# A second norm computed earlier, a weight form queued sooner, and a 32-byte shift moved from one product unit to another

## The chip, the cores and the metric

The kernel runs on one core of a Trainium2 chip. A core has five engines with queues of their own: PE (TensorE, matrix products), DVE (VectorE), ACT (ScalarE), POOL (GpSimd) and SP (SyncE, which here issues DMAs). Each works through its instructions in the order of the program and waits at semaphores for the others. The metric is the device time of one execution in microseconds (us), as a median of several runs.

## The reference

One decoder block in float32, 512 tokens by 1024 features: a gated linear attention and a sparse attention in parallel, merged and added to the input, and then the channel mixer. The change lies in the channel mixer and in the norm ahead of it:

```python
x = x + rms_norm(mixed @ w_out[l], norm_mix_post[l])
h = rms_norm(x, norm_ffn_pre[l])                      # the "second norm"
f = (jax.nn.silu(h @ w_ffn_gate[l]) * (h @ w_ffn_up[l])) @ w_ffn_down[l]
x = x + rms_norm(f, norm_ffn_post[l])
```

`w_ffn_gate` and `w_ffn_up` have 2816 columns, 22 blocks of 128.

## The kernel before

Every float32 operand of a product is split into a high part (rounded by a cast) and a low part (the rest), and a product is three matmuls: high by high, high by low, low by high. Features lie on the partitions, in eight tiles k = 0 to 7; tokens lie on the free axis, in two halves e = 0 and 1 of 256.

**The second norm.** `resid(e)` adds the mixers' output to the input. For each k VectorE multiplies (L1424, one input in PSUM) and adds (L1425), ScalarE makes the high part (L1426) and VectorE the low part (L1427). `resid_squares(e)` then squares each tile on ScalarE (L1436) and adds the eight squares up on GpSimd (L1439). `norm2_sums(e)` sums over the partitions with two matmuls of one column (L251; the trace shows each float32 one as two), turns the mean into a reciprocal root on VectorE (L259) and GpSimd (L260), and `norm2_scale(e)` spreads it over the partitions by matmuls (L268) and copies it to `rb_x` on ScalarE (L1450). `normed(e)` multiplies the tiles by it on VectorE (L1608, eight instructions).

**Column blocks 0 to 2, "plain".** The first two (weights `w0` and `w1`, gate and up) run in halves of tokens by `ffn_half` (L1462 to L1464, 48 matmuls for a half), since the products with the unscaled `x` need no norm: the scale is applied behind them. The third uses all 512 tokens at once (L226 to L228, accumulators `third`).

**Column blocks 3 to 21, "units".** From N0 = 3 on a unit replaces the 8 half-size products of a block by 7 (a Strassen-like scheme): a11, s2, s3, s1, a12, a22, s4, named after their weights, each 4 x 3 = 12 matmuls of 256 columns (L1662). VectorE adds the results (L1668, into `us` and `wk`). The weights of a11 and a12 are the gate's two halves (`prep_g`), that of a22 the up's second half (`prep_u`), s1 to s4 are sums of quarters. Their high parts are cast on ScalarE, and the low parts are made by a negated copy and a DMA on GpSimd's queue that adds the weight from memory (`dma_split`). The other operands are `b11`, `b12`, `b21`, `b22` (half e of `nb`) and four differences of them, split by `x_form` (L1617). N0 and N0+1 have only two banks each, of two regions; the matmuls of s1 write the same bank as those of s2, from which the first L1668 reads.

A scheduler puts the instructions in order on each engine, from its own costs and from the places in the program; `tc.issue_after(x)` keeps an instruction behind another one, which may be on another engine. `SHIFT` is 16 and `TURN` 8 elements of four bytes: they set the addresses at which a form of weights begins.

The lines of the program that set the order here are these (before):

```python
    high_end, _ = resid(1, marks[-1])
    ffn_half(0, w0, first, range(5, 8))
    resid_squares(1, range(KD), None, high_end)
    ...
    normed(0)
    x_form("b11", [(b11, *at(0))])
    ffn_half(1, w1, second, range(0, 6))
    scale_made = norm2_sums(1)
    ffn_half(1, w1, second, range(6, 8))
```

Of the kernel before, what the change touches and what calls it, by code (L numbers as in the profile page):

```python
# [11 lines left out]
AF = mybir.ActivationFunctionType  # L12
OP = mybir.AluOpType
# [5 lines left out]
KD = D // 128  # L19
# [14 lines left out]
SHIFT = 16  # L34
TURN = 8
# [98 lines left out]
def hybrid_block_kernel(ctx: ExitStack, tc: tile.TileContext, I, outT):  # L134
    nc = tc.nc
    act, dve, pool, pe = nc.scalar, nc.vector, nc.gpsimd, nc.tensor
# [29 lines left out]
    g_fpre, g_fpost = vecs[:, 16:24], vecs[:, 24:32]  # L166
# [5 lines left out]
    rb_x = base.tile([128, S], F32, name="rb_x")  # L172
# [25 lines left out]
    for key in with_gla + with_cmp + with_att + late:  # L198
        kind, n = key
# [19 lines left out]
    def prod(ps, w, xh, xl, k0, kn, ktot, t=ALL):  # L219

        wh, wl = w
        marks = []
        for kk in range(kn):
            k = k0 + kk
            c = slice(kk * 128, (kk + 1) * 128)
            pe.matmul(ps[:, t], wh[:, c], xh(k)[:, t], start=(k == 0), stop=False)  # L226
            pe.matmul(ps[:, t], wh[:, c], xl(k)[:, t], start=False, stop=False)  # L227
            marks.append(pe.matmul(ps[:, t], wl[:, c], xh(k)[:, t], start=False, stop=(k == ktot - 1)))  # L228
        return marks
# [32 lines left out]
    broadcast, queued = [], {}  # L262
# [13 lines left out]
    for k in range(KD):  # L276
# [3 lines left out]
        if k == 0:  # L280
            act.activation(out=warm, in_=mhalf[:, 0:1], func=AF.Exp)
        last = act.activation(out=hT[:, k, :], in_=X[:, k], func=AF.Copy, scale=g_pre[:, k:k + 1])
        dve.scalar_tensor_tensor(out=hTl[:, k, :], in0=X[:, k], scalar=g_pre[:, k:k + 1],
                                 in1=hT[:, k, :].bitcast(F32), op0=OP.mult, op1=OP.subtract)
# [48 lines left out]
    halves = (slice(0, S // 2), slice(S // 2, S))  # L333
# [205 lines left out]
    for c in range(4):  # L539
        w = tk.next(("tok", 0, c))  # L540
# [78 lines left out]
    for j in range(NP):  # L619
# [6 lines left out]
        after = queued["dve"]  # L626
# [713 lines left out]
    def uu_half():  # L1340
        uturn[0] += 1
        return uub[:, 0:1024] if uturn[0] % 2 else uub[:, 1024:2048]
# [6 lines left out]
    def w_slot(which, shift=SHIFT):  # L1349

        if which == "w":
            return regions.next(shift)
        if which == "c":
            t = hlc(F32R, "w_hl")
            return [t[:, c:c + 1024] for c in (SHIFT, 1024 + SHIFT)]
        if which == "u":
            return uu_half(), uu_half()
        if which in ("d0", "d1"):
            t = wpair(which)
            return t[:, 0:1024], t[:, 1024:2048]  # L1360
        return tuple(wtile(t) for t in {"g3": ("g3h", "g3l"), "rw": ("rw", "rw")}[which])
# [6 lines left out]
    h2h, h2l = quads("h2h", 4, F32R, "hh"), quads("h2l", 2, F32R, "hl")  # L1368
    h2l23 = hlc(F32R, "h2l23")[:, 0:2048].rearrange("p (b a t) -> p b a t", b=2, a=2)
    h2l += [h2l23[:, i] for i in range(2)]  # L1370
    x1 = [slot(k) for k in range(8)]
# [41 lines left out]
    def resid(e, after=None, ks=range(KD), mult_after=None):  # L1413

        t = halves[e]
        if e not in rb_of:
            rb_of[e] = over_partitions(rs1, "tp", blocks[e], after)
        rb = rb_of[e]
        for k in ks:
            i, j = k // 2, k % 2  # L1420
            y = x1[k][:, t]
            hi, lo = h2h[i][:, j, t], h2l[i][:, j, t]
            with tc.issue_after(mult_after.ins) if mult_after else nullcontext():
                dve.tensor_tensor(out=y, in0=y, in1=rb[:, t], op=OP.mult)  # L1424
            dve.tensor_tensor(out=y, in0=y, in1=xs[i][:, j, t], op=OP.add)  # L1425
            last = act.activation(out=hi, in_=y, func=AF.Copy, scale=g_fpre[:, k:k + 1])  # L1426
            end = dve.scalar_tensor_tensor(out=lo, in0=y, scalar=g_fpre[:, k:k + 1], in1=hi.bitcast(F32),  # L1427
                                           op0=OP.mult, op1=OP.subtract)
        return last, end

    def resid_squares(e, ks=range(KD), after=None, squared_after=None):
        t = halves[e]
        for k in ks:
            sq = sq2[0][:, t] if k == 0 else sq2[1 + (k - 1) % 6 // 2][:, halves[(k - 1) % 2]]
            with tc.issue_after(squared_after.ins) if squared_after else nullcontext():
                act.activation(out=sq, in_=x1[k][:, t], func=AF.Square)  # L1436
            if k > 0:
                with tc.issue_after(after.ins) if after else nullcontext():
                    pool.tensor_tensor(out=sq2[0][:, t], in0=sq2[0][:, t], in1=sq, op=OP.add)  # L1439

    rs2 = ffn.tile([128, NT], F32, name="rs2")

# [5 lines left out]
    def norm2_scale(e, after):  # L1448
        ps = over_partitions(rs2, "tp", blocks[e], after)
        return act.copy(rb_x[:, halves[e]], ps[:, halves[e]])  # L1450

    def ffn_half(e, w, ps, ks=range(KD)):

        t = halves[e]
        marks = []
        for k in ks:
            i, j = k // 2, k % 2
            c = slice(k * 128, (k + 1) * 128)
            for x in range(2):
                wh, wl = w[x]  # L1460
                o = ps[x][:, t]
                pe.matmul(o, wh[:, c], h2h[i][:, j, t], start=(k == 0), stop=False)  # L1462
                pe.matmul(o, wh[:, c], h2l[i][:, j, t], start=False, stop=False)
                last = pe.matmul(o, wl[:, c], h2h[i][:, j, t], start=False, stop=(k == KD - 1))  # L1464
            marks.append(last)
        return marks
# [34 lines left out]
    N0 = NPLAIN  # L1501
# [29 lines left out]
        return minus  # L1531

    def prep_g(n, after=None):
        hi, lo = w_slot(("w", "g3", "w")[(n - N0) % 3], SHIFT + (TURN if n == N0 + 3 else 0))
        minus = dma_split(n, hi, lo, raws[n, "w_gate"], I["w_gate"][n], after)
        forms[n, "a11"], forms[n, "a12"] = [(hi[:, c], lo[:, c]) for c in (slice(0, 512), slice(512, 1024))]
        return minus

    def prep_u(n, after=None, t=None):
        t = uu_half() if t is None else t  # L1540
        hi, lo = t[:, 0:512], t[:, 512:1024]
        dma_split(n, hi, lo, ups[n][:, 512:1024], I["w_up"][n, :, 512:1024], after)
        forms[n, "a22"] = (hi, lo)
# [59 lines left out]

    XF = {}

    def normed(e):
        for k in range(KD):
            dve.scalar_tensor_tensor(out=nb[k // 4][e][:, k % 4, :], in0=x1[k][:, halves[e]], scalar=g_fpre[:, k:k + 1],  # L1608
                                     in1=rb_x[:, halves[e]], op0=OP.mult, op1=OP.mult)

    def x_form(name, segs, after=None):

# [144 lines left out]
    for n in (6, 7):  # L1757
        out_half(n, 1)
    sq2 = [t[:, i, :] for t in quads("sq2_", 2, F32, "e") for i in range(2)]
# [4 lines left out]
    on_act, on_dve = resid(0, None, range(KD - 1, KD), queued["mean"])  # L1764
    resid_squares(0, range(3, KD), root)
    marks = ffn_half(0, w0, first, range(3, 5))
    high_end, _ = resid(1, marks[-1])
    ffn_half(0, w0, first, range(5, 8))
    resid_squares(1, range(KD), None, high_end)
    split_pair(N0, s12, ("s1", "s2"), on_act, True)  # L1770
    w1 = (st.next(("g", 1)), st.next(("u", 1)))
    second = (bank("mm"), bank("mm"))
# [3 lines left out]
    marks = ffn_half(1, w0, first, range(0, 2))  # L1776
    norm2_scale(0, marks[-1])
    ffn_half(1, w0, first, range(2, 8))
    nb = [[ffn.tile([128, 4, 256], F32, tag="a%d" % (2 * p + e), name="nb%d%d" % (p, e)) for e in range(2)]
          for p in range(2)]  # L1780
    b11, b12, b21, b22 = [t.rearrange("p q t -> p (q t)") for t in (nb[0][0], nb[0][1], nb[1][0], nb[1][1])]
    normed(0)
    x_form("b11", [(b11, *at(0))])
    ffn_half(1, w1, second, range(0, 6))
    scale_made = norm2_sums(1)
    ffn_half(1, w1, second, range(6, 8))
    third = (bank("acc"), bank("acc"))

    def h2(p):
        return lambda k: p[k // 2][:, k % 2, :]  # L1790

    w2 = st.next(("g", 2))
    marks = prod(third[0], w2, h2(h2h), h2(h2l), 0, 3, KD)
    rb_made = norm2_scale(1, marks[-1])
    x_form("b21", [(b21, flat(quad("e0", F32R, "x4h")), flat(quad("e1", F32R, "x4l")))])
    normed(1)
    prod(third[0], [x[:, 384:1024] for x in w2], h2(h2h), h2(h2l), 3, 5, KD)
# [19 lines left out]
    for n in range(N0, KF):  # L1817
        if n + 2 < KF:
            load(n + 2, "w_gate")
            load(n + 2, "w_up")  # L1820
        last = unit(n, rest_of_forms if n == N0 else None,
                    (lambda copied: prep_u(N0 + 2, copied, uu_next)) if n == N0 + 2 else None)
        if n == N0:
            end = last
        if n == N0 + 1:
            plain_end()
            plain_out(2, *third)()
        if n + 1 < KF:
            prep_st(n + 1, end, plain_outs if n == N0 else None)
        if n + 2 < KF:  # L1830
            prep_g(n + 2, {N0 + 1: queued.get("s1cast"), N0 + 2: queued.get(("s34", N0 + 2)),
                           N0 + 3: queued.get(("s12", N0 + 4))}.get(n))
            if n == N0 + 1:
                uu_next = uu_half()
            if n > N0:
                prep_u(n + 2, queued["s1cast"] if n == N0 + 1 else None)
        if 2 * KH <= n < 2 * KH + 4:
            down_t3(n - 2 * KH)
# [352 lines left out]
```

## Time and profile before

| what | value |
|---|---|
| median of 3 runs | 822.71 us (822.53 to 822.76) |
| the profiled execution's own time | 822.37 us |
| its span, first to last instruction | 820.6 us |
| granted TensorE clock | 1.000 |
| w1's second half begins on PE | 497.26 us |
| first unit (N0) begins on PE | 514.71 us |
| N0+4 begins on PE | 554.83 us |

A row of the timeline gives the start and the length in us, the engine, the line, the operation, the tiles written and read, the shape, how many instructions were merged, and in square brackets how long the engine was idle just before and what released it. The length of a matmul includes its way through the array; what counts for the time is the distance from one start to the next. Line numbers in the profile and below are those of the kernel before, unless they are said to be those of after.

### The profile page before, as it was taken

How to read it: one execution, taken by the hardware profiler on the slowest of the kernel's cores; microseconds unless marked ns; L12 is line 12 of the kernel's file. 1: busy time of each engine (PE TensorE's matmuls, PEld its weight loads, DVE VectorE, ACT ScalarE, POOL GpSimd, SP SyncE). 2: the span in 40 equal slices, each digit the busy share in tenths (PEclk: the TensorE clock that was granted, in tenths of full speed). 3: DMA queues.
4: the chain of work that ended last, by engine and by line, in shares of the span. 5: the costliest groups of instructions: out<-in, count | busy, mean ns of one | idle time of the engine just before them, and what ended most of it. 6: DMA issues, size and time to landing. Idle time of an engine off the chain costs nothing.

```text
span 820.6 us, 14977 instructions
## 1 busy us (share of the span) xinstructions
PE 813.5 (99%) x5676; PEld 750.2 (91%) x5676; DVE 649.5 (79%) x1219; ACT 523.6 (64%) x954; POOL 177.4 (22%) x221
## 2 busy tenths in 40 slices
PE   9999999999999999999999999999999999999997
PEld 8999999988888888888888999999999999889996
DVE  7878889955678988877675387997888778939885
ACT  7666697646536778887545577677655667536453
POOL 0242222312311111111001355012211110001264
PEclk9999999999999999999999999999999999999999
DMA  7588888411233354444238759589788882335323
GB/s 259 139 219 205 183 182 191 103 52 51 92 125 98 96 116 119 111 105 103 55 110 303 227 125 259 102 229 224 185 192 193 199 196 67 101 92 181 91 103 103
DMA packets 45449, 120.75 MB, mean 147 GB/s; under 512 B 5981, under 2 KB 11373, under 8 KB 45249
## 3 DMA queue, kind: packets, MB, share of 16 engines
q1 hardware_dynamic: 30576, 82.40, 30.1%
q0 software_dynamic: 14080, 36.76, 25.4%
q8 instruction: 44, 0.72, 0.3%
q10 hardware_dynamic: 720, 0.64, 0.2%
q14 instruction: 29, 0.23, 0.1%
HBM read 105.10 MB, written 4.19 MB: 133 GB/s over the span
## 4 chain that ended last, share of the span: by engine, by line
PE 93%; DVE 3%; ACT 2%; issue 1%; DMA 0%; SPq 0%; DVEq 0%; ACTq 0%
PE ps_sc L1662 7%; PE ps_mm L226 7%; PE ps_mm L227 6%; PE ps_mm L228 6%; PE ps_acc L1662 5%; PE ps_mm L1662 4%; PE ps_mm L446 4%; PE ps_tp L446 4%; PE ps_tp L1662 4%; PE ps_sc L1993 4%; PE ps_sc L446 3%; PE ps_acc L446 3%; PE ps_tp L1172 2%; PE ps_mm L1993 2%; PE ps_sc L227 1%; PE ps_sc L228 1%
## 5 line engine op out<-in xcount | busy, mean ns | idle before, releaser
L99 ACT CAST wbuf<-wraw 128x1024 fp32r<-128x1024 f32 (+3 forms) x56 | 54.1, 967 | 45.2 <-issue 11.1
L226 PE MATMUL ps_mm<-hT_hi,wbuf 128*128 128x512 f32 x152 | 61.8, 407 | 0.0
L106 DVE TENSOR_TENSOR wbuf<-wraw,wbuf 128x1024 fp32r<-128x1024 f32 (+3 forms) x41 | 44.3, 1082 | 20.6 <-ACT wbuf L99 16.3
L227 PE MATMUL ps_mm<-hT_lo,wbuf 128*128 128x512 f32 x152 | 60.0, 394 | 0.0
L228 PE MATMUL ps_mm<-hT_hi,wbuf 128*128 128x512 f32 x152 | 59.8, 394 | 0.0
L1548 ACT CAST w_d<-s 128x1024 fp32r<-128x1024 f32 x25 | 26.1, 1045 | 30.3 <-PE ps_acc L1662 13.9
L1131 ACT ACTIVATE p<-p,mx 128x512 f32<-128x512 f32 (+1 forms) x64 | 35.8, 560 | 9.2 <-DVE mx L1129 8.4
L244 DVE TENSOR_TENSOR pl<-ps_tp,ph 128x512 fp32r<-128x512 f32 (+1 forms) x64 | 31.2, 490 | 9.7 <-ACT ph L243 8.8
L1129 DVE CUSTOM_DVE_ANT_0 p<-ps_sc,causal 128x512 f32<-128x512 f32 (+1 forms) x64 | 30.0, 485 | 7.4 <-PE ps_sc L1122 7.2
L228 PEld LDWEIGHTS ps_mm<-hT_hi,wbuf 128*128 128x128 f32 x152 | 28.5, 188 | 6.5 <-DVE wbuf L106 0.4
L226 PEld LDWEIGHTS ps_mm<-hT_hi,wbuf 128*128 128x128 f32 x152 | 28.6, 188 | 5.5
L103 POOL DMA_DIRECT2D wbuf<-wraw x15 | 13.1, 875 | 94.3 <-ACT wbuf L102 94.3
L227 PEld LDWEIGHTS ps_mm<-hT_lo,wbuf 128*128 128x128 f32 x152 | 28.7, 189 | 4.5
L1530 POOL DMA_DIRECT2D wbuf<-in_w_gate x13 | 11.1, 856 | 89.1 <-ACT wbuf L1528 71.8
L243 ACT CAST ph<-ps_tp 128x512 fp32r<-128x512 f32 (+1 forms) x64 | 26.4, 414 | 6.1 <-PE ps_tp L1172 5.3
L1555 DVE TENSOR_TENSOR w_d<-s,w_d 128x1024 fp32r<-128x1024 f32 x24 | 29.3, 1220 | 0.0
L1172 PE MATMUL ps_tp<-ident,p 128*128 128x128 f32 x160 | 27.7, 272 | 0.0
L1172 PEld LDWEIGHTS ps_tp<-ident,p 128*128 128x128 f32 x160 | 20.8, 140 | 7.1
L226 PE MATMUL ps_mm<-gla_hi,wbuf 128*128 128x512 f32 x64 | 26.1, 407 | 0.0
L227 PE MATMUL ps_mm<-gla_lo,wbuf 128*128 128x512 f32 x64 | 25.2, 393 | 0.0
L228 PE MATMUL ps_mm<-gla_hi,wbuf 128*128 128x512 f32 x64 | 25.1, 393 | 0.0
L1548 ACT CAST w_hl<-s 128x1024 fp32r<-128x1024 f32 x11 | 11.5, 1046 | 18.2 <-PE ps_acc L1662 7.0
(981 smaller groups left out, 3210.5 us busy)
## 6 DMA issues: line engine op xcount, KB each, us to landing
wraw<-in_w_t SPq DMA_DIRECT2D x28, 512.0 KB, 3.6
wraw<-in_w_gate SPq DMA_DIRECT2D x21, 512.0 KB, 5.6
rw<-in_w_up SPq DMA_DIRECT2D x19, 512.0 KB, 6.7
wbuf<-wraw POOLq DMA_DIRECT2D x15, 512.0 KB, 4.5
wbuf<-in_w_gate POOLq DMA_DIRECT2D x13, 512.0 KB, 5.5
urw<-in_w_t SPq DMA_DIRECT2D x12, 512.0 KB, 5.5
uub<-in_w_up POOLq DMA_DIRECT2D x19, 256.0 KB, 7.3
raw<-in_w_down SPq DMA_DIRECT2D x10, 448.0 KB, 3.3
```

Source lines behind the costliest of these rows:

```text
L99: self.cast = self.nc.scalar.copy(hi[:, :cols], raw[:, :cols])
L106: self.nc.vector.tensor_tensor(out=lo[:, :cols], in0=raw[:, :cols], in1=hi[:, :cols].bitcast(F32), op=OP.subtract)
L226: pe.matmul(ps[:, t], wh[:, c], xh(k)[:, t], start=(k == 0), stop=False)
L227: pe.matmul(ps[:, t], wh[:, c], xl(k)[:, t], start=False, stop=False)
L228: marks.append(pe.matmul(ps[:, t], wl[:, c], xh(k)[:, t], start=False, stop=(k == ktot - 1)))
L244: return dve.tensor_tensor(out=lo, in0=src, in1=hi.bitcast(F32), op=OP.subtract)
L446: pe.matmul(o, w[:, c], x_of(b, q, low), start=(first and q == 0 and i == 0), stop=(q == 3 and i == 2), skip_group_check=True)
L1131: act.activation(out=o, in_=o, func=AF.Exp, scale=-1.0, bias=mx[:, i:i + 1], accum_out=z[:, i:i + 1])
L1172: queued["turn"] = pe.transpose(tp[:, i * 128:(i + 1) * 128], p[:, OFF[i] + k * 128:OFF[i] + (k + 1) * 128], ident)
L1548: cast = act.copy(hi, t)
L1662: last = pe.matmul(o, w[:, c], x[q], start=(first and q == 0 and i == 0), stop=(q == 3 and i == 2), skip_group_check=True)
L1993: pe.matmul(o, c, x[q], start=(first and n == 0 and i == 0), stop=(n == KH - 1 and i == 2), skip_group_check=True)
```

## The change

1. `resid_squares(1, ...)` becomes `second_squares(low_end)`. ScalarE squares tiles 0 to 3 right behind the sixth high part, and tiles 4 to 7 behind the eighth. GpSimd adds three of the squares in place of seven; VectorE adds the other four (three adds L1451 and a last one L1453 in the changed kernel), behind the last low part of `resid(1)`; `normed(0)` comes behind these.
2. The sums `norm2_sums(1)` stand ahead of w1's second half (before: behind six of its eight tiles), and `norm2_scale(1)` behind three of its tiles (before: behind three tiles of the third block).
3. The form a22 of N0+2 is asked for in unit N0+1, behind its copy of the first product, and not in unit N0+2.
4. The gate's form of N0 begins 32 bytes further, and that of N0+3 no longer does.

```diff
@@ resid
-            last = act.activation(out=hi, in_=y, func=AF.Copy, scale=g_fpre[:, k:k + 1])
+            last = queued["high", e, k] = act.activation(out=hi, in_=y, func=AF.Copy, scale=g_fpre[:, k:k + 1])
...
+    def second_squares(low_end):
+        t = halves[1]
+        sq = [sq2[0][:, t]] + [sq2[1 + (k - 1) % 6 // 2][:, halves[(k - 1) % 2]] for k in range(1, KD)]
+        for k in range(KD):
+            with tc.issue_after(queued["high", 1, 5 if k < 4 else 7].ins):
+                act.activation(out=sq[k], in_=x1[k][:, t], func=AF.Square)
+            if 0 < k < 4:
+                pool.tensor_tensor(out=sq[0], in0=sq[0], in1=sq[k], op=OP.add)
+            elif k > 4:
+                with tc.issue_after(low_end.ins):
+                    low_end = dve.tensor_tensor(out=sq[4], in0=sq[4], in1=sq[k], op=OP.add)
+        with tc.issue_after(low_end.ins):
+            queued["squares"] = dve.tensor_tensor(out=sq[0], in0=sq[0], in1=sq[4], op=OP.add)
...
-        hi, lo = w_slot(("w", "g3", "w")[(n - N0) % 3], SHIFT + (TURN if n == N0 + 3 else 0))
+        hi, lo = w_slot(("w", "g3", "w")[(n - N0) % 3], SHIFT + (TURN if n == N0 else 0))
...
-    def prep_u(n, after=None, t=None):
-        t = uu_half() if t is None else t
+    def prep_u(n, after=None):
+        t = uu_half()
...
-    high_end, _ = resid(1, marks[-1])
+    _, low_end = resid(1, marks[-1])
     ffn_half(0, w0, first, range(5, 8))
-    resid_squares(1, range(KD), None, high_end)
+    second_squares(low_end)
...
-    normed(0)
+    normed(0, queued["squares"])
     x_form("b11", [(b11, *at(0))])
-    ffn_half(1, w1, second, range(0, 6))
     scale_made = norm2_sums(1)
-    ffn_half(1, w1, second, range(6, 8))
+    marks = ffn_half(1, w1, second, range(0, 3))
+    rb_made = norm2_scale(1, marks[-1])
+    ffn_half(1, w1, second, range(3, 8))
...
-    marks = prod(third[0], w2, h2(h2h), h2(h2l), 0, 3, KD)
-    rb_made = norm2_scale(1, marks[-1])
+    prod(third[0], w2, h2(h2h), h2(h2l), 0, 3, KD)
...
-                    (lambda copied: prep_u(N0 + 2, copied, uu_next)) if n == N0 + 2 else None)
+                    (lambda copied: prep_u(N0 + 2, copied)) if n == N0 + 1 else None)
...
-            if n == N0 + 1:
-                uu_next = uu_half()
```

The order on VectorE from the end of `resid(1)` to the sums' mean (L259), before. The tiles `slot` hold the sum with the input, `h2l` its low part, `sq` the squares, `nb` the normed tiles, `rs` the mean:

```order
L1427 SCALAR_TENSOR_TENSOR h2l_4804<-slot_4812,vecs,h2h_4801 128x256
L1608 SCALAR_TENSOR_TENSOR nb_5531<-slot_4805,vecs,rb_x 128x256
L1608 SCALAR_TENSOR_TENSOR nb_5531<-slot_4806,vecs,rb_x 128x256
L1608 SCALAR_TENSOR_TENSOR nb_5531<-slot_4807,vecs,rb_x 128x256
L1608 SCALAR_TENSOR_TENSOR nb_5531<-slot_4808,vecs,rb_x 128x256
L1608 SCALAR_TENSOR_TENSOR nb_5533<-slot_4809,vecs,rb_x 128x256
L1608 SCALAR_TENSOR_TENSOR nb_5533<-slot_4810,vecs,rb_x 128x256
L1608 SCALAR_TENSOR_TENSOR nb_5533<-slot_4811,vecs,rb_x 128x256
L1608 SCALAR_TENSOR_TENSOR nb_5533<-slot_4812,vecs,rb_x 128x256
L1617 TENSOR_TENSOR hT_lo<-nb_5531,hT_hi 128x1024
L259 TENSOR_SCALAR rs_4943<-ps_tp 128x2
```

And after, the same stretch (L1623 is `normed`, L1632 `x_form` in the changed kernel):

```order
L1427 SCALAR_TENSOR_TENSOR h2l_4804<-slot_4812,vecs,h2h_4801 128x256
L1451 TENSOR_TENSOR sq_1_5282<-sq_1_5282 128x256 x2
L1451 TENSOR_TENSOR sq_1_5282<-sq_1_5282,sq_0_5281 128x256
L1453 TENSOR_TENSOR sq_0_5281<-sq_0_5281,sq_1_5282 128x256
L1623 SCALAR_TENSOR_TENSOR nb_5531<-slot_4805,vecs,rb_x 128x256
L1623 SCALAR_TENSOR_TENSOR nb_5531<-slot_4806,vecs,rb_x 128x256
L1623 SCALAR_TENSOR_TENSOR nb_5531<-slot_4807,vecs,rb_x 128x256
L1623 SCALAR_TENSOR_TENSOR nb_5531<-slot_4808,vecs,rb_x 128x256
L1623 SCALAR_TENSOR_TENSOR nb_5533<-slot_4809,vecs,rb_x 128x256
L1623 SCALAR_TENSOR_TENSOR nb_5533<-slot_4810,vecs,rb_x 128x256
L1623 SCALAR_TENSOR_TENSOR nb_5533<-slot_4811,vecs,rb_x 128x256
L259 TENSOR_SCALAR rs_4943<-ps_tp 128x2
```

Four adds have come between the low part and the norm's first half, and L259 has moved ahead of the norm's last tile and of the first split of `b11`.

VectorE around N0's first additions, before (`w_d` and `s` belong to weight forms; `x_1`, `x_3` and `x5l` are low parts of the last two other operands, for a22 and s4):

```order
L1617 TENSOR_TENSOR hT_lo<-nb_5531,hT_hi 128x1024
L1668 TENSOR_TENSOR us<-ps_tp,us 128x256
L1617 TENSOR_TENSOR x5l<-nb_5533,x5h 128x1024
L1668 TENSOR_TENSOR us<-ps_tp,us 128x256
L1617 TENSOR_TENSOR x_1_5771<-nb_5534,x_0_5770 128x512
L1617 TENSOR_TENSOR x_3_5773<-nb_5534,x_2_5772 128x512
L1668 TENSOR_TENSOR wk<-ps_tp,us 128x256
L1564 TENSOR_TENSOR s_5833<-rw 128x512
L1565 TENSOR_TENSOR s_5833<-s_5833,wraw 128x512
```

And after (L1683 is the addition L1668, L1578 and L1579 are L1564 and L1565):

```order
L1632 TENSOR_TENSOR hT_lo<-nb_5531,hT_hi 128x1024
L1632 TENSOR_TENSOR x_1_5771<-nb_5534,x_0_5770 128x512
L1632 TENSOR_TENSOR x_3_5773<-nb_5534,x_2_5772 128x512
L1632 TENSOR_TENSOR x5l<-nb_5533,x5h 128x1024
L1578 TENSOR_TENSOR s_5833<-rw 128x512
L1579 TENSOR_TENSOR s_5833<-s_5833,wraw 128x512
L1683 TENSOR_TENSOR us<-ps_tp,us 128x256
```

The three splits and two sums now stand ahead of N0's first addition, on which N0's s1 waits.

TensorE around the sums L251, before (`ps_mm` is the bank of w1's products):

```order
L1462 MATMUL ps_mm<-h2h_4800,uub 128x256
L1463 MATMUL ps_mm<-h2l_4804,uub 128x256
L1464 MATMUL ps_mm<-h2h_4800,uub 128x256
L251 MATMUL ps_tp<-consts,sq_0_5281 128x1 x2
L1462 MATMUL ps_mm<-h2h_4801,w_g3h 128x256
```

And after, where L1476 to L1478 are `ffn_half` and `ps_sc` is the bank of w0's products:

```order
L1476 MATMUL ps_sc<-h2h_4801,wbuf 128x256
L1477 MATMUL ps_sc<-h2l_4804,wbuf 128x256
L1478 MATMUL ps_sc<-h2h_4801,wbuf 128x256
L251 MATMUL ps_tp<-consts,sq_0_5281 128x1 x2
L1476 MATMUL ps_mm<-h2h_4798,w_g3h 128x256
```

The sums have moved from behind the 36th matmul of w1's second half to its start; L268 has moved from behind the ninth matmul of the third block to behind the 18th of this half.

TensorE at the start of N0, before; N0 writes `ps_tp` and N0+1 `ps_sc`:

```order
L1662 MATMUL ps_tp<-hT_lo,wbuf 128x256
L1662 MATMUL ps_tp<-hT_hi,wbuf 128x256
L1662 MATMUL ps_tp<-hT_hi,w_d_5409 128x256
L1662 MATMUL ps_sc<-hT_hi,w_g3h 128x256
L1662 MATMUL ps_sc<-hT_lo,w_g3h 128x256
L1662 MATMUL ps_sc<-hT_hi,w_g3l 128x256
L1662 MATMUL ps_tp<-hT_lo,w_d_5409 128x256
```

And after, at the same place:

```order
L1677 MATMUL ps_tp<-hT_lo,wbuf 128x256
L1677 MATMUL ps_tp<-hT_hi,wbuf 128x256
L1677 MATMUL ps_tp<-hT_hi,w_d_5409 128x256
L1677 MATMUL ps_tp<-hT_lo,w_d_5409 128x256
L1677 MATMUL ps_tp<-hT_hi,w_d_5409 128x256 x2
```

N0+1's first matmuls no longer stand inside N0: its a11 comes behind N0's last product, and the units up to N0+3 likewise follow one another.

More of the change, by code (lines that the diff above doesn't have):

```diff
@@ L1604, in hybrid_block_kernel, with normed @@
     XF = {}
-    def normed(e):
+    def normed(e, after=None):
         for k in range(KD):
-            dve.scalar_tensor_tensor(out=nb[k // 4][e][:, k % 4, :], in0=x1[k][:, halves[e]], scalar=g_fpre[:, k:k + 1],
-                                     in1=rb_x[:, halves[e]], op0=OP.mult, op1=OP.mult)
+            with tc.issue_after(after.ins) if after else nullcontext():
+                dve.scalar_tensor_tensor(out=nb[k // 4][e][:, k % 4, :], in0=x1[k][:, halves[e]], scalar=g_fpre[:, k:k + 1],
+                                         in1=rb_x[:, halves[e]], op0=OP.mult, op1=OP.mult)
     def x_form(name, segs, after=None):
```

## The prediction

> **What bounds the kernel now.** I read the page's totals and its chain first, then stretches of equal work, then rows in order of time around each edit.
>
> ```profile
> span 820.6 us, 14977 instructions
> ...
> PE 813.5 (99%) x5676; PEld 750.2 (91%) x5676; DVE 649.5 (79%) x1219; ACT 523.6 (64%) x954; POOL 177.4 (22%) x221
> ...
> PE 93%; DVE 3%; ACT 2%; issue 1%; DMA 0%; SPq 0%; DVEq 0%; ACTq 0%
> ```
>
> TensorE is busy 99% of the span and carries 93% of the chain, so an edit counts only where it moves a TensorE start. The next view gives TensorE's busy time (instructions), clock, DMA share and GB/s in three stretches: the plain products from the start of w1's second half to the first unit, units N0 to N0+3, and the four units after.
>
> ```profile
> 497.26:514.71 17.45, 17.45 (x106) 1.00 0.97 259
> 514.71:554.83 40.12, 39.48 (x338) 1.00 0.68 167
> 554.83:592.91 38.08, 38.08 (x339) 1.00 0.88 211
> ```
>
> Both unit stretches hold 4 x 84 = 336 products at clock 1.00 (the counts include rows across an edge). The later four take 38.08, or 113.3 ns each; the first four take 40.12. These 2.04 us are all that the units here can give back. Where they go, TensorE in order of time (start, length, line, output<-inputs):
>
> ```profile
> 514.71 0.28 PE L1662 MATMUL ps_tp<-hT_hi,wbuf 128*128 128x256 f32 x1
> ...
> 516.12 0.28 PE L1662 MATMUL ps_tp<-hT_hi,w_d 128*128 128x256 f32 x1
> ...
> 530.33 0.29 PE L1662 MATMUL ps_mm<-hT_lo,wbuf 128*128 128x256 f32 x1
> 531.25 0.39 PE L1662 MATMUL ps_sc<-hT_hi,w_hl 128*128 128x256 f32 x1 [0.64 <-DVE us L1668]
> ...
> 550.66 0.28 PE L1662 MATMUL ps_mm<-x4h,wbuf 128*128 128x256 f32 x1
> ...
> 552.10 0.28 PE L1662 MATMUL ps_acc<-x5h,uub 128*128 128x256 f32 x1
> ...
> 741.21 0.28 PE L1993 MATMUL ps_sc<-db,wbuf 128*128 128x256 f32 x1
> ...
> 743.67 0.39 PE L1993 MATMUL ps_sc<-w_d,w_g3h 128*128 128x256 f32 x2
> 743.90 0.28 PE L1993 MATMUL ps_sc<-w_d,w_g3l 128*128 128x256 f32 x1
> 744.01 0.39 PE L1993 MATMUL ps_sc<-w_d,w_g3h 128*128 128x256 f32 x2
> ```
>
> One stall, 530.33 to 531.25, loses 0.92 - 0.11 = 0.81: interleaved products wait for VectorE's add. The twelve products of N0's first block take 1.41 (117.5 ns each, after a change from 512 to 256 columns), 0.05 above the fast rate. The N0+3 block with weights moved 32 bytes, 550.66 to 552.10, takes 120 ns each, 0.08 in twelve. Two such blocks and the first one make 0.2; the remaining 1.0 is smaller gaps of about 0.1 where one unit's products are mixed into another's.
>
> **The change part by part, 1: the second norm.** TensorE around its sums (L251) and its broadcast (L268), then VectorE, ScalarE and GpSimd:
>
> ```profile
> 497.26 0.28 PE L1462 MATMUL ps_mm<-h2h,w_g3h 128*128 128x256 f32 x1
> ...
> 501.34 0.50 PE L251 MATMUL ps_tp<-consts,sq 128*128 128x1 f32 x4
> 501.70 0.36 PE L1462 MATMUL ps_mm<-h2h,w_g3h 128*128 128x256 f32 x1
> ...
> 505.29 0.61 PE L268 MATMUL ps_tp<-ident,rs 128*128 128x128 f32 x4
> 505.66 0.48 PE L226 MATMUL ps_acc<-h2h,w_d 128*128 128x512 f32 x1
> ```
> ```profile
> 492.17 0.74 DVE L1424 TENSOR_TENSOR slot<-slot,ps_tp 128x256 f32<-128x256 f32 x2
> 492.83 0.75 DVE L1425 TENSOR_TENSOR slot<-slot,xs 128x256 f32<-128x256 f32 x2
> 493.83 0.88 DVE L1427 SCALAR_TENSOR_TENSOR h2l<-slot,vecs,h2h 128x256 fp32r<-128x256 f32 x2 [0.24 <-ACT h2h L1426]
> 496.95 5.32 DVE L1608 SCALAR_TENSOR_TENSOR nb<-slot,vecs,rb_x 128x256 f32<-128x256 f32 x8 [2.23 <-ACT rb_x L1450]
> ...
> 503.33 0.14 DVE L259 TENSOR_SCALAR rs<-ps_tp 128x2 f32<-128x2 f32 x1
> ...
> 506.35 3.26 DVE L1608 SCALAR_TENSOR_TENSOR nb<-slot,vecs,rb_x 128x256 f32<-128x256 f32 x8 [1.39 <-ACT rb_x L1450]
> ...
> 519.80 0.42 DVE L1668 TENSOR_TENSOR us<-ps_tp,us 128x256 f32<-128x256 f32 x1
> 520.14 1.21 DVE L1617 TENSOR_TENSOR x5l<-nb,x5h 128x1024 fp32r<-128x1024 f32 x1
> ...
> 524.47 0.69 DVE L1585 TENSOR_TENSOR s<-wraw,rw 128x512 f32<-128x512 f32 x1
> ```
> ```profile
> 494.11 2.55 ACT L1436 ACTIVATE sq<-slot 128x256 f32<-128x256 f32 x8
> 496.56 0.35 ACT L1450 COPY rb_x<-ps_tp 128x256 f32<-128x256 f32 x1
> ...
> 500.23 1.05 ACT L1616 CAST hT_hi<-nb 128x1024 fp32r<-128x1024 f32 x1 [2.17 <-DVE nb L1608]
> 501.19 1.05 ACT L1528 ACTIVATE wbuf<-rw 128x1024 fp32r<-128x1024 f32 x1
> ...
> 505.94 0.37 ACT L1450 COPY rb_x<-ps_tp 128x256 f32<-128x256 f32 x1 [1.71 <-PE ps_tp L268]
> ```
> ```profile
> 490.38 1.16 POOL L260 TENSOR_TENSOR rs<-rs,consts 128x2 f32<-128x2 f32 x1 [2.08 <-DVE rs L259]
> 491.50 0.87 POOL L103 DMA_DIRECT2D we<-wraw  x1
> ...
> 496.54 3.38 POOL L1439 TENSOR_TENSOR sq<-sq,sq 128x256 f32<-128x256 f32 x4
> 499.99 0.80 POOL L1439 TENSOR_TENSOR sq<-sq 128x256 f32<-128x256 f32 x1
> ...
> 503.55 0.71 POOL L260 TENSOR_TENSOR rs<-rs,consts 128x2 f32<-128x2 f32 x1 [2.75 <-DVE rs L259]
> ```
>
> *Removed:* four of GpSimd's seven adds. These end at 500.79 and L251 stands at 501.34, so nothing waits for them today; by themselves they are worth nothing.
>
> *The three adds that stay* start when the DMA issue of 491.50 is over, about 492.4, and now run beside L1425 and L1427. The same eight VectorE instructions L1608 took 5.32 beside GpSimd's adds and 3.26 alone. In that time GpSimd ran about four and a half adds (496.95 to 500.79 at 0.845), so one add costs VectorE 2.06 / 4.5 = 0.46. Three cost 1.4, less the 0.24 that VectorE idles at 493.83 anyway and about 0.3 of the first add, which falls beside L1424 (its second input is PSUM). I take 0.85; the bounds are 0 and three whole adds, 2.5. L1427 then ends at 494.71 + 0.85 = 495.55.
>
> *Added:* four dependent adds on VectorE. The nearest rows are L1425 and L1427, 0.41 to 0.44; dependent ones follow at that full length: 4 x 0.43 gives squares at 497.25. ScalarE is no limit: its last four squares (0.32 each) follow the last high part at 494.8, and end at 496.1. TensorE reaches L251 at 497.26: no wait, at most 0.6 if VectorE is held up longer.
>
> *L251 to L268.* L251 takes 0.36 (to 501.70). The eighteen products behind it, at N0's first rate of about 118 ns and with 0.1 to restart, put TensorE at L268 at 497.3 + 0.36 + 0.1 + 18 x 0.118 = 499.9. The sums must pass VectorE in that time, where L259 stands behind seven instructions of the first half's norm, 497.2 + 7 x 0.395 = 499.95, then 0.14; GpSimd's L260 takes 0.71 to 1.16. L268 starts at 500.9 to 501.3. **A new wait of 1.0 to 1.4, I take 1.2**, 0.1 of it restart included; 0.2 if the adds cost VectorE nothing. The first unit starts at 514.71 + 1.2 = 515.9.
>
> *What comes earlier:* the copy to rb_x. On ScalarE it stands behind the cast of hT_hi (ready with the fourth L1623, 498.8) and three instructions spaced 0.96 as 500.23 to 501.19: 498.8 + 4 x 0.96 + 0.35 = 503.0 in place of 506.31. VectorE's second half of the norm starts 3.3 earlier.
>
> **2: the units.** N0's products are no longer mixed with N0+1's, and N0+2's no longer with N0+3's first ones, so the 2.04 is open. But s1 of N0 comes sooner and carries a wait for the first addition into us (L1668, now L1683), whose PSUM bank it writes. In VectorE's new order that addition stands behind x_1, x_3, x5l and two sums for N0+1. Today 506.35 to 519.80 is 13.45 without idle time; x5l up to 524.47 is another 4.33, of which two more additions into us and wk take 0.34 each: 3.65. So it starts at 503.0 + 13.45 + 3.65 = 520.1 and ends at 520.5, and s1 starts at 520.6. TensorE would be there at 515.9 + 12 x 0.120 + 24 x 0.1133 = 520.1: **a second new wait of 0.5**, plus 0.1 of slow restart. Behind s1 I find VectorE and ScalarE ahead of TensorE by 0.2 to 0.6 throughout N0+1: 300 products at 113.3 ns, 34.0, and 0.08 for the second shifted block. The units end at 520.7 + 34.0 + 0.1 = 554.8, against 554.83.
>
> The rows show three rates for one shape: 113.3, 117.5 and 120 ns. The Trainium skill ("TensorE: Matmul & The Clock Gate", section Back-to-back issue gap) has a single one, N / 2.4 + 2.5 ns, an estimate of 109.2 at 256 columns: by it the shifted blocks and the slow first block would cost nothing, the sum would be 0.2 lower, and rival (c) could not be. The rows differ from it, and are kept.
>
> **3: the a22 form of N0+2** is issued one unit earlier: two ScalarE instructions (0.63 each at this size by the rate of L1528's rows) and a GpSimd DMA. SP's queue keeps its order; GpSimd, 22% busy, is passed without a wait; the form's product is more than 5 us off. Nothing, unless ScalarE is late for N0+1's copy; then 0.2.
>
> **4: the shift** costs N0's two blocks what N0+3's cost, 0.08 each: 0.
>
> Sum: +1.2 and +0.6 of waits, +0.2 of rates already in the units' time, against 2.04: 0.0, between -0.8 (no conflict between GpSimd and VectorE) and +1.1. Since VectorE's chain sets s1, 1.7 of wait at L268 would be absorbed. The profiled execution took 822.37, 0.34 below the median of 822.71, with the same sum on both: **822.7**.
>
> **Rivals.** (a) *The gain comes whole:* L268 and s1 both find their inputs. That needs VectorE 1.2 sooner at L259 and 0.6 at s1: 822.7 - 1.9 = 820.8. For it: L259 may be issued earlier than I place it. Against: seven instructions ahead of it, each 0.395. 0.08.
>
> (b) *Each add holds VectorE for its whole length*, 0.845 and not 0.46: 1.15 more. L251 then waits 1.1, rb_x comes at 504.1 and s1 at 521.7: +1.1, 823.8. For it: the adds' rows are that long. Against: L1608's mean beside them is 0.67, not 1.24. 0.12. The Trainium skill ("SBUF — State Buffer", section SBUF: two separate sides) has the pair of ports locked for a whole instruction, the loser fully blocked, which reads like (b); the rows agree only if half of an add's recorded length is itself waiting.
>
> (c) *The slow rate stays, slower than before:* the shifted block of N0+3 is the last thing that brings the rate to 113.3 before the long run of units (741.21 to 743.67 ran 21 products at 117; behind them 744.01 - 743.67 = 0.34 for three is fast). Without it at N0+3, a wait that left the rate slow would cost 4.4 ns on each of some 1,280 products up to about 696: +5.6, 828.3. It decides if any wait in the first four units ends slow; the stall at 531.25 did not. 0.05.
>
> (d) *The change doesn't do what it says*, the norm being held back elsewhere: L268 waits over 2.5, +0.8 and more; inside (b)'s range, 0.03.
>
> **How the numbers follow.** The forecast holds 0.72, (a) 0.08, (b) 0.12, (c) 0.05, (d) 0.03. The range, 821.6 to 823.9, takes in the conflict's lower bound (-0.8, with 0.3 for the scatter of the runs) and (b); it leaves out (a), (c) and half of (d). 0.2% is 1.65, about what a measurement tells from no change: only (a), within 821.06, is faster, 0.09 with a little of the lower bound; (c) and a tail of (b) and (d) are slower, 0.09; the rest is 0.82.
>
> **What would show it.** Right: L251 at about 497.3 without a wait, L268 idle about 1 us behind GpSimd's L260, N0's s1 idle about 0.5 behind VectorE's L1683, no 0.64 stall, the units in 38.9 from a start at 515.9, and 113.3 ns at 560. Wrong: L1425 and L1427 not stretched beside GpSimd; products at 117 ns behind 555; a new wait in N0+1.

## The result, and the profile after

The changed kernel takes 830.89 us (median of 6 executions, 826.12 to 833.91) where the kernel before takes 822.74: a ratio of 1.0087, 95% interval 1.0070 to 1.0104. The profiled execution took 831.05, its span is 829.3, 8.7 more than before. The prediction of 822.7 and its range to 823.9 were wrong; the rival that it called (c), with 0.05, is what happened, beside two smaller losses. Below, 113.3 ns from one start to the next in a stream of 256-column products is called the fast rate, 117.8 ns the slow rate.

The page's totals and chain after:

```profile
span 829.3 us, 14989 instructions
...
PE 820.8 (99%) x5676; PEld 757.6 (91%) x5676; DVE 650.7 (78%) x1223; ACT 524.0 (63%) x954; POOL 178.0 (21%) x217
...
PE 94%; DVE 2%; issue 2%; POOL 1%; DMA 0%; ACT 0%; SPq 0%; POOLq 0%; ACTq 0%; DVEq 0%
```

TensorE is busy 7.3 us longer with the same 5676 instructions: most of the loss is no wait, but slower products.

One thing has to be taken off first. TensorE's first products of the program run at half rate for a while, and how long differs from profile to profile, though all kernels here have the same first products. Before, and then after (TensorE in order of time):

```profile
5.15 0.63 PE L342 MATMUL ps_mm<-wbuf,hT_hi 128*128 128x440 f32 x2 [0.72 <-DVE wbuf L93]
5.62 0.56 PE L342 MATMUL ps_sc<-wbuf,hT_hi 128*128 128x440 f32 x2
6.02 0.56 PE L343 MATMUL ps_mm<-wbuf,hT_lo 128*128 128x440 f32 x2
```

```profile
5.17 1.07 PE L342 MATMUL ps_mm<-wbuf,hT_hi 128*128 128x440 f32 x2 [0.46 <-DVE wbuf L93]
6.04 0.92 PE L342 MATMUL ps_sc<-wbuf,hT_hi 128*128 128x440 f32 x2
6.77 0.58 PE L343 MATMUL ps_mm<-wbuf,hT_lo 128*128 128x440 f32 x2
```

The first row's two products take 0.87 up to the next start after (5.17 to 6.04), and 0.47 before. From there on the same products start 0.75 later, and stay so up to the norm. In the other thirteen profiles of this case this amounts to 0 to 2.4 us against the one of before, so two profiles are compared below with it taken off ("less the start"); medians carry it as scatter.

What is left is read from the stretches between the same products in both kernels: w0's last product to N0, the units N0 to N0+3, and the four units behind them. After:

```profile
498.00:518.26 20.26, 18.00 (x106) 1.00 0.98 240
518.26:557.53 39.27, 39.27 (x337) 1.00 0.75 171
557.53:597.11 39.58, 39.58 (x339) 1.00 0.79 193
```

N0 begins at 518.26 - 0.74 = 517.5, 2.8 later than before (514.71). The units N0 to N0+3 take 39.27 in place of 40.12, 0.85 less. And the four units behind them, with no wait in either kernel, take 39.58 in place of 38.08: 336 products at 117.8 ns, not 113.3. That rate holds up to the last unit, where the loss of this stretch has grown to 5.6. With 0.4 in what follows, which arises among the program's last products: 0.74 + 2.8 - 0.85 + 5.6 + 0.4 = 8.7.

One of the six executions took 826.12, some 5 less than the rest. No profile of it was kept; by its time alone it looks like one that kept the fast rate.

### The profile page after: what moved, and what is told of

Same layout as the page of the kernel before. It is cut to its first block, busy times and chain, and to the rows that moved or that the text cites. A ratio compares the mean times of both kernels' runs of the same rounds, so it can differ in the third digit from the quotient of the medians.

```text
span 829.3 us, 14989 instructions
## 1 busy us (share of the span) xinstructions
PE 820.8 (99%) x5676; PEld 757.6 (91%) x5676; DVE 650.7 (78%) x1223; ACT 524.0 (63%) x954; POOL 178.0 (21%) x217
## 4 chain that ended last, share of the span: by engine, by line
PE 94%; DVE 2%; issue 2%; POOL 1%; DMA 0%; ACT 0%; SPq 0%; POOLq 0%; ACTq 0%; DVEq 0%
PE ps_sc L1677 7%; PE ps_mm L226 6%; PE ps_mm L227 6%; PE ps_mm L228 6%; PE ps_acc L1677 5%; PE ps_tp L1677 5%; PE ps_mm L1677 5%; PE ps_mm L446 4%; PE ps_tp L446 4%; PE ps_sc L2006 4%; PE ps_sc L446 3%; PE ps_acc L446 3%; PE ps_tp L1172 2%; PE ps_mm L2006 2%; PE ps_acc L227 2%
## 5 line engine op out<-in xcount | busy, mean ns | idle before, releaser
L1683 DVE TENSOR_TENSOR wk<-ps_acc,us 128x256 f32<-128x256 f32 x24 | 10.1, 423 | 18.1 <-PE ps_acc L1677 17.7
```

## The slow rate: the experiments on the shift

In the profile after, N0's second shifted block ends at 113.3 ns, as it should. Then this stands in N0+1:

```profile
533.38 0.28 PE L1677 MATMUL ps_sc<-hT_hi,w_hl 128*128 128x256 f32 x1
533.50 0.29 PE L1677 MATMUL ps_sc<-x5h,uub 128*128 128x256 f32 x1
533.62 0.28 PE L1677 MATMUL ps_sc<-x5l,uub 128*128 128x256 f32 x1
533.74 0.40 PE L1677 MATMUL ps_sc<-x5h,uub 128*128 128x256 f32 x2
533.98 0.28 PE L1677 MATMUL ps_sc<-x5l,uub 128*128 128x256 f32 x1
```

The product of 533.50 takes some 15 ns more than its neighbours (0.29 for 0.28; the next start stands 128 ns behind it in the trace's nanoseconds). In the program it waits for VectorE's second addition into us (L1683), which ended at 532.93 + 0.42 = 533.35. From 533.62 on the distance from start to start is 0.12, not 0.113, and no shifted block follows that could end it.

**shift_back** puts the shift back where it was.

```diff
-        hi, lo = w_slot(..., SHIFT + (TURN if n == N0 else 0))
+        hi, lo = w_slot(..., SHIFT + (TURN if n == N0 + 3 else 0))
```

> The changed kernel with the shift of 32 bytes back at N0+3 and none at N0; the order of all instructions is the same. Theory of the rate: a wait of 15 ns in N0+1 leaves TensorE at 117.7 ns a product, and only a shifted block brings 113.3 back, so N0+3's blocks end it: the 1,280 products behind them gain 4.4 ns each, 5.6 us, and the time is about 825.3, with the long run of units at 113.3. Theory of the waits (the norm's sums came too early, and the time went there): about 830.9, no change.

Measured: 826.69 (824.77 to 828.45), ratio 1.0040 [1.0025, 1.0055]. Its profile, the first four units and the next four:

```profile
519.32:558.68 39.36, 39.36 (x338) 1.00 0.73 171
558.68:596.76 38.08, 38.08 (x339) 1.00 0.82 201
```

The slow rate runs from N0 up to N0+3, whose shifted blocks end it: 38.08 behind them. Part 4 of the change cost 4.2 us of median. The median is 1.4 above the 825.3 expected. The profile, 826.21, began with 1.8 of slow start, and four of the six executions have a mean clock of 0.998, of which more below.

**shift_both** has it at both places (`TURN if n in (N0, N0 + 3) else 0`).

> The changed kernel with the shift at N0 and at N0+3. Theory of the rate: N0+3's blocks end the slow rate as in the kernel with the shift there alone, so 825.3, within 0.4 of it; what N0's shift gives besides is the second half of N0 and N0+1 at 113.3, 0.4 us at most. Theory of the waits: about 830.9.

825.94 (825.43 to 827.69), ratio 1.0034 [1.0021, 1.0047]. The wait of 15 ns is there in its profile too, the rate falls to 117.8 behind it, and at N0+3 it rises again.

**shift_only** and **no_shift** take the kernel before and move the shift to N0, or drop it (`SHIFT` alone). No instruction changes its place.

> The kernel before, with only the shift moved from N0+3 to N0. If the shift is a reset that is needed only behind a wait that ends slow, then the stalls of the kernel before, of which ten of ten ended fast in its trace, leave nothing to reset: 822.7, with 113.3 ns in the long run. If losing the shift at N0+3 is enough by itself for the slow rate: 822.7 + 5.6 = 828.3.

> The kernel before with no shift in any unit; nothing else differs. If the loss of N0+3's shift is what leaves the slow rate standing: most executions at about 828.3, with 117.7 ns through the long run, and some at 822.8, as with the shift moved to N0. If the shift at N0 itself brings the slow rate: 822.8 in all.

The eight executions of shift_only took 822.76 and 823.02 in two, and 828.22 to 830.39 in six. Those of no_shift took 822.41 to 825.13 in six and 828.15 to 830.81 in four. The profile of shift_only is one of the slow ones. Two of its stalls matter here, a short one in N0+1 and then the long one; the kernel before has both too. The rows of both, then three stretches of 12 products each: ahead of the short stall, between the two, and behind the long one (columns as above: stretch, its length, TensorE's busy time and count, granted clock, DMA share, GB/s; the counts include rows across an edge):

```profile
527.41 0.28 PE L1662 MATMUL ps_sc<-hT_lo,w_d 128*128 128x256 f32 x1
527.53 0.47 PE L1662 MATMUL ps_sc<-hT_hi,w_d 128*128 128x256 f32 x2
527.83 0.28 PE L1662 MATMUL ps_sc<-hT_lo,w_d 128*128 128x256 f32 x1
...
531.16 0.39 PE L1662 MATMUL ps_sc<-hT_hi,w_hl 128*128 128x256 f32 x1 [0.58 <-DVE us L1668]
```
```profile
524.55:525.91 1.36, 1.36 (x15) 1.00 0.00 0
528.77:530.19 1.42, 1.42 (x15) 1.00 0.00 0
532.45:533.86 1.41, 1.41 (x15) 1.00 1.01 209
```

The rate falls at the short stall of 0.07 (184 ns between the two starts that are merged in the row of 527.53), and the long one leaves it slow. In the kernel before, the same two stalls (198 ns and 0.92 us from start to start) both end at 113.3. In no_shift's profile the rate is slow up to the long stall, and that stall brings it back:

```profile
533.12 0.39 PE L1662 MATMUL ps_sc<-hT_hi,w_hl 128*128 128x256 f32 x1 [0.51 <-DVE us L1668]
```
```profile
530.80:532.21 1.41, 1.41 (x14) 1.00 0.00 0
534.37:535.73 1.36, 1.36 (x14) 1.00 1.12 226
```

Without a block at N0+3 that brings it back, shift_only's slow rate lasts through the units:

```profile
514.63:555.10 40.47, 39.89 (x338) 1.00 0.70 171
555.10:594.67 39.57, 39.57 (x338) 1.00 0.86 201
```

So the same wait, in the same order of instructions, leaves the rate fast in some executions and slow in others. The times of shift_only, in two groups, point to the same within one program, though no profile of its shorter executions was kept. The kernel before has only 822.4 to 826.1 in all its executions; its N0+3 blocks come behind its last stall. The loss of the shift at N0+3 is enough for the slow rate: without any shift both outcomes are there. Whether the shift at N0 adds to it, six of eight against four of ten can't tell.

**sum_later** takes the wait of 15 ns away and leaves the shift at N0.

```diff
-        with tc.issue_after(queued["sum2"].ins) if n == N0 + 3 else nullcontext():
+        with tc.issue_after(queued["sum2"].ins) if n in (N0 + 2, N0 + 3) else nullcontext():
```

> The changed kernel with one difference sum for N0+2 on VectorE held behind the other, so that the second addition into us of N0+1, behind which TensorE waits 15 ns, runs 0.6 us sooner (one product of N0+2 also moves ahead of N0+1's last block). Theory of the rate, with that wait as the place where it falls: no wait, the rate stays at 113.3 from N0's second shifted block on, and the time is 830.9 - 5.8 = 825.1. If the slow rate comes from somewhere else, or from any later wait: 830.9.

827.33 (825.43 to 830.48), ratio 1.0047 [1.0029, 1.0064]. In its profile (825.43) that wait is gone, a new one of 0.2 in two products stands at 537.27 behind the product that moved, it ends fast, and the four units behind N0+3 take 38.08. The 825.1 expected was missed: three other executions took 827.3 to 828.1, about the scatter that slow starts give (long_wait's seven span 2.6), but one took 830.48. One wait less does not make the kernel safe. In long_wait's profile (below) the wait of N0+1 is there, with 126 ns from start to start, and there it ends fast. Which way a wait ends, no run here shows beforehand.

## The late start: the experiments on the norm

VectorE after, from the end of `resid(1)`, then GpSimd and TensorE:

```profile
493.54 1.50 DVE L1425 TENSOR_TENSOR slot<-slot,xs 128x256 f32<-128x256 f32 x2
494.96 1.35 DVE L1427 SCALAR_TENSOR_TENSOR h2l<-slot,vecs,h2h 128x256 fp32r<-128x256 f32 x2
496.24 0.95 DVE L1451 TENSOR_TENSOR sq<-sq 128x256 f32<-128x256 f32 x2
497.30 0.42 DVE L1451 TENSOR_TENSOR sq<-sq,sq 128x256 f32<-128x256 f32 x1
497.82 0.42 DVE L1453 TENSOR_TENSOR sq<-sq,sq 128x256 f32<-128x256 f32 x1
498.17 2.85 DVE L1623 SCALAR_TENSOR_TENSOR nb<-slot,vecs,rb_x 128x256 f32<-128x256 f32 x7
500.94 0.15 DVE L259 TENSOR_SCALAR rs<-ps_tp 128x2 f32<-128x2 f32 x1
501.00 0.48 DVE L1623 SCALAR_TENSOR_TENSOR nb<-slot,vecs,rb_x 128x256 f32<-128x256 f32 x1
501.40 1.22 DVE L1632 TENSOR_TENSOR hT_lo<-nb,hT_hi 128x1024 fp32r<-128x1024 f32 x1
```
```profile
501.17 2.02 POOL L260 TENSOR_TENSOR rs<-rs,consts 128x2 f32<-128x2 f32 x1 [5.54 <-DVE rs L259]
```
```profile
498.30 0.61 PE L251 MATMUL ps_tp<-consts,sq 128*128 128x1 f32 x4
...
503.25 0.71 PE L268 MATMUL ps_tp<-ident,rs 128*128 128x128 f32 x4 [2.11 <-POOL rs L260]
```

Less the start (0.74), VectorE's low parts end at 495.57, its squares at 497.50, L259 starts at 500.20: within 0.3 of the sum. Then GpSimd's L260, two columns, takes 2.02 where 0.71 and 1.16 were the rows of before. It was issued while VectorE had an L1623 in work and the split L1632 of 1.22 next in its queue, and it ended 0.57 behind the end of that split. TensorE waits 2.11 for it. From the last product's start ahead of L268 (500.86) to L268's own 2.39 pass, 2.28 more than the 0.11 of the fast rate; with 0.3 at L251 (0.42 from the last product's start) and 0.1 each in the matmuls of L251 and L268 this is the 2.8.

**power_alone** keeps that split out of L260's way: on VectorE it comes behind the split of b21, everything else as in shift_both.

```diff
-    x_form("b11", [(b11, *at(0))])
+    b11h, b11l = at(0)
+    act.copy(b11h, b11)
...
+    with tc.issue_after(split21.ins):
+        dve.tensor_tensor(out=b11l, in0=b11, in1=b11h.bitcast(F32), op=OP.subtract)
```

> The changed kernel with the shift at N0 and N0+3, and the long split of b11 on VectorE (1.22 us, two inputs in SBUF) held behind that of b21, so that GpSimd's L260 does not run beside it. If L260's 2.02 us is a wait for that split: L260 takes 0.7 to 1.2, L268 waits 0.9 to 1.3 in place of 2.1, no stretch at half clock, 823.5 to 824.4. If 2.02 is L260's own length there: 825.9 and a wait of 2.1.

825.66 (823.34 to 826.60), ratio 1.0015 [1.0002, 1.0028]; the 823.5 to 824.4 expected was missed, with five executions at 823.3 to 823.7 and seven at 825.6 to 826.6. L260 and L268 in its profile:

```profile
502.68 0.89 POOL L260 TENSOR_TENSOR rs<-rs,consts 128x2 f32<-128x2 f32 x1 [5.53 <-DVE rs L259]
```
```profile
503.63 0.71 PE L268 MATMUL ps_tp<-ident,rs 128*128 128x128 f32 x4 [1.04 <-POOL rs L260]
```

L260 falls to 0.89 and the wait to 1.04, so 2.02 was a wait for VectorE's split and not L260's own length. This profile began with 2.2 us of slow start; less the start its units begin at 516.42, 1.1 earlier than after. The Trainium skill ("SBUF — State Buffer", section SBUF: two separate sides) has a VectorE instruction with two SBUF inputs and a GpSimd instruction that reads SBUF exclude each other for a whole instruction; these rows agree.

**The half clock.** In shift_both's profile TensorE comes back from the same wait (2.18) at 502.81, and 1.4 us later this stands (columns: stretch, its length, TensorE's busy time and count, granted clock, DMA share, GB/s):

```profile
502.80:504.20 1.40, 1.39 (x12) 1.00 0.48 195
504.20:507.60 3.40, 3.40 (x19) 0.50 0.75 198
507.60:509.00 1.40, 1.40 (x11) 0.99 1.07 196
```

For 3.4 us the clock is 0.50 and a product of 256 columns takes 213 ns: 16 products, 1.5 us lost. The profile of after shows clock 1.00 there, but three of its six executions have a mean clock of 0.998 or less; 3.4 us at half are 0.002 of the span. A mean alone doesn't prove such a stretch, since the clock also falls at the program's end: 8 of 75 executions of the kernel before have 0.998 or less.

**long_wait** makes the wait longer, with L268 behind 12 products (`range(0, 2)` and `range(2, 8)`).

> The changed kernel with the shift at N0 and N0+3, and L268 behind 12 products in place of 18, so that its wait grows from 2.1 to 2.8 us. If the half clock behind it comes from the idle share of some window of about 3.4 us, that falls in most executions now: 3.4 us at clock 0.50 behind L268, 826 or more. If it has nothing to do with the wait, it comes in about as many profiles as before, and the time is 825.4 to 826.2.

826.27 (826.04 to 828.66), ratio 1.0043 [1.0028, 1.0057]. The wait is 2.86, and the mean clock is 0.997 or 0.998 in all seven executions. With the wait of 2.1 (after, shift_back, shift_both, sum_later) it is 0.998 or less in 17 of 25, and in power_alone, with a wait of 1.04, in one of twelve. Long_wait's profile:

```profile
502.81 0.71 PE L268 MATMUL ps_tp<-ident,rs 128*128 128x128 f32 x4 [2.86 <-POOL rs L260]
```
```profile
504.10:507.50 3.40, 3.40 (x19) 0.50 0.45 135
```

So the half clock goes with the length of the wait: not sure at 2.1, in all seven at 2.9. The traces also show what differs between the profiles at 2.1. In all fourteen, the stretches at clock 1.00 and those at 0.50 inside the program last whole multiples of 3.413 us, counted from where the clock first rises (146 such windows up to the fall in shift_both, sum_later and long_wait). Of the window just ahead of the fall TensorE was idle 2.00, 1.99 and 2.14 us in these three. In after, shift_back and norm_only a window's edge splits the same wait of 2.1, at most 1.51, 1.61 and 1.59 fall into one window, and the clock holds behind it. The Trainium skill ("TensorE: Matmul & The Clock Gate", section Part 1: The HAM clock gate) has the clock fall after an idle window of about 3.4 us; the length of the window agrees, but here 2.0 us of idle time in it were enough, and the measurement decides.

**late_both** takes the wait away by time: L268 behind 36 products (`range(0, 6)` and `range(6, 8)`), shift at both places.

> The changed kernel with the shift at N0 and N0+3, and L268 behind 36 products of w1's second half in place of 18. Theory: L268's wait of 2.1 us, and the stretch of half clock that follows it in some executions (3.4 us, 16 products at 213 ns, 1.6 us), are what the earlier norm costs. TensorE then reaches L268 when its input is there, no wait and clock 1.00; the first unit starts some 2 us sooner. If VectorE's additions for N0 are in time, the units keep their gain of 2 us: 821.2. If VectorE's chain ends N0's s1 instead: 823.6.

**adds_first** adds to it that N0's first addition comes ahead of the last three splits on VectorE (`lo_after=added`).

> As the kernel with L268 behind 36 products, and besides N0's first addition on VectorE comes ahead of the splits x_1, x_3 and x5l. If s1 of N0 waits for VectorE there, this takes the wait away: 821.2, and up to 1.2 less than without. If it does not wait: the same time.

824.51 (822.30 to 825.03), ratio 1.0007 [0.9998, 1.0016], and 824.39 (823.09 to 825.57), ratio 1.0008 [0.9998, 1.0018]. Neither waits over 0.2 at L268, and neither at N0's s1, so the order of the additions isn't what costs. N0 begins at 515.5 less the start, 2.0 sooner than after and as expected. But the units take 39.1 and 39.6, not 38.1: other waits of 0.1 to 0.5 appear in them, and N0's first five blocks run at 117.8. Less the start late_both ends 0.15 ahead of the kernel before; the 821.2 that I expected is not there.

**squares_only** is part 1 and 3 without part 2: the sums and L268 at their old places, the shift at N0+3.

> The changed kernel with the sums and L268 at their old places, the shift at N0+3 as before; the squares by ScalarE, GpSimd and VectorE and the earlier a22 form stay. If the earlier places of L251 and L268 are what costs: 822.7, within 0.4. If the four adds on VectorE or the earlier form cost by themselves: 824 or more.

823.79 (823.33 to 825.49), ratio 1.0004 [0.9995, 1.0013]. The adds on VectorE cost nothing to be measured: less the start (0.52) N0 begins at 514.70, before at 514.71. Its units take 40.9, with one stall of 1.18 for VectorE, longer than before.

**norm_only** is parts 1 and 2 without part 3: the a22 form of N0+2 is queued late again, the shift at N0+3.

> The changed kernel with the shift at N0+3 alone and the a22 form of N0+2 queued late, as before: parts 1 and 2 alone. If part 3 costs nothing: as the kernel with only the shift undone, 825.5 to 826.7, the long run at 113.3. If the earlier form is what makes TensorE wait in N0+1: 0.3 less and no wait of 15 ns there.

835.20 (833.97 to 835.56), ratio 1.0137 [1.0121, 1.0154]: 8.5 us more than shift_back, and neither of the two outcomes that I had written down. TensorE in N0+2 (and the stretch behind the wait), then GpSimd's issue of N0+2's form in norm_only and in shift_back:

```profile
553.20 0.80 PE L1677 MATMUL ps_sc<-x5h,uub 128*128 128x256 f32 x2 [6.34 <-DMA uub<-in_w_up]
```
```profile
553.20:558.60 5.40, 5.40 (x25) 0.50 0.01 2
```
```profile
543.88 0.86 POOL L1544 DMA_DIRECT2D uub<-in_w_up  x1 [0.99 <-ACT uub L1542]
```
```profile
532.77 0.86 POOL L1544 DMA_DIRECT2D uub<-in_w_up  x1 [2.89 <-ACT uub L1542]
```

Without part 3 the DMA for N0+2 is issued at 543.88, 11 us later, TensorE waits 6.3 for it, and behind the wait 25 products run at half clock, some 2.4 more. The form is queued behind the copy of N0+2's first product, which ScalarE makes at 542.17 in norm_only; the cast follows at 542.43. In the kernel before N0+2's first products stood among those of N0+1, the copy came early, and the cast starts at 530.68. With parts 1 and 2 the scheduler no longer mixes the units, and then the form must be queued sooner. Part 3 is not free of effect; it avoids a loss that comes with parts 1 and 2 (which of the two does it was not tried: squares_only leaves out part 2, but has part 3).

**best** puts together what helped: the shift at both places, L251 behind six products and L268 behind 30 more.

```diff
+    ffn_half(1, w1, second, range(0, 1))
     scale_made = norm2_sums(1)
-    marks = ffn_half(1, w1, second, range(0, 3))
+    marks = ffn_half(1, w1, second, range(1, 6))
     rb_made = norm2_scale(1, marks[-1])
-    ffn_half(1, w1, second, range(3, 8))
+    ffn_half(1, w1, second, range(6, 8))
```

> The changed kernel with the shift at N0 and N0+3, L251 behind the first six products of w1's second half and L268 behind 30 more: no wait at either, clock 1.00, the units' gain kept. Measured from the same product at the start of the norm, 0.3 less than with L251 at the start of the half, 0.5 less than the kernel before; as a median 822.2 to 823.2, less than the scatter of single executions.

823.22 (822.23 to 825.23), ratio 1.0000 [0.9989, 1.0011]. Its profiled execution took 822.27:

```profile
515.84:554.73 38.89, 38.82 (x338) 1.00 0.72 176
554.73:592.81 38.08, 38.08 (x338) 1.00 0.84 208
```
```profile
502.86 0.71 PE L268 MATMUL ps_tp<-ident,rs 128*128 128x128 f32 x4 [0.65 <-POOL rs L260]
```

The units keep 1.2 of gain, L251, L268 and the 0.65 of wait take 1.0 of it. Less the start it ends 0.2 ahead of the kernel before, which medians can't tell from nothing. It beats the changed kernel clearly and the kernel before not.

## Why the prediction was wrong

**Part 4, "0", and rival (c), 0.05.** This is the step that failed. The shift was priced by what its own twelve products cost, 0.08, and not by what it ends. The price of (c) was right, 5.6 forecast and 5.6 in the profile. Its chance was not: it rested on stalls of a single execution that ended fast, above all that of 531.25. In the profile of shift_only a shorter one of them ends slow and that of 531.25 doesn't mend it, and by their times six of eight and four of ten executions are slow without N0+3's shift. That N0+3's blocks are the last reset ahead of some 1,280 products was written in the prediction; that a reset is worth most where the state ahead of it is not always the same was not drawn from it.

**The wait at L268, 1.2.** It was 2.1 (2.3 with the restart), with 0.3 at L251, where the sum had none. The term that was mis-sized is L260, put at 0.71 to 1.16 and 2.02 here. The sum counted GpSimd's adds against VectorE, and did not count VectorE's split against GpSimd. N0 began 2.8 later, not 1.2.

**Half clock.** Not in the sum at all; 1.5 us in the executions that have it. The wait of 2.1 was taken to cost its length.

**The second wait, 0.5 at N0's s1.** Not there after: TensorE came later than VectorE. The chain of VectorE itself was late by 0.7 to 1.0 (the second half of the norm at 504.40 less 0.74 = 503.7, forecast 503.0; the first addition's end at 521.5 less the start, forecast 520.5).

**Right:** the adds' conflict (L1427 ended at 495.57 less the start, forecast 495.55; rival (b) would have been 1.15 later), the squares (497.50, 497.25).

**Right by luck:** the units N0 to N0+3, 39.27 where 38.9 was forecast. The 0.6 forecast at s1 was not there, and about 1.2 of slow rate was, of which the sum had 0.2.

**Part 3, "nothing":** no run has it alone; norm_only shows that without it the other parts cost 8.5 us more, which the sum didn't see.

## What to carry to other kernels

Something that costs 0.1 us and has no visible effect may be what ends a state: before moving it, ask what the state ahead of it is in every execution, not in the one that was profiled, and what runs behind it. A wait is priced with what comes after it, the rate and the clock, and not by its length alone. And where two engines share a port, a short instruction on the critical path is priced by the long instruction that it may have to wait for: L260 took 0.89 and 2.02 here.

## What the runs showed of the hardware that I had not expected

A wait of 15 ns in a stream of 256-column products was followed by 117.8 ns a product in place of 113.3, for 5.6 us of loss from N0+4 to the last unit; the same wait, at 13 ns, ended at 113.3 in long_wait. A stall of 0.9 us left the rate fast in before and slow in shift_only, and brought it from slow to fast in no_shift. Twelve products with weights moved 32 bytes, entered at the slow rate, were followed by 113.3 in all twelve cases inside the units: N0+3's first block in shift_back, shift_both and power_alone, and N0's second block in the nine profiles with the shift at N0. N0's first block, right behind the 512-column products, left it slow in all nine. A wait of 2.1 us was followed by 3.4 us at half clock in two of five profiles, those in which 2.0 us of it fell into one window of 3.413 us; where at most 1.61 did, the clock held. And the slow start differs by up to 2.4 us between profiles; the kernel before's executions scatter from 822.4 to 826.1, so it may be most of that, which no profile of a slower execution of it shows.
